# Three ways to split weights: adding transfers in place of VectorE subtractions in a decoder layer, and a new order on GpSimd

## The chip, the core and the metric

The kernel runs on one core of one Trainium2 chip. Its five engines work from queues of their own: TensorE (PE in the profile; PEld its weight loads), VectorE (DVE), ScalarE (ACT), GpSimd (POOL) and SyncE (SP, which here only issues transfers). The metric is the device time of one launch in microseconds (us). An engine runs its instructions strictly in the order of its queue: one that waits holds up all that stand behind it.

## The reference

One layer of a decoder trunk, in float32, on 256 prompt positions and 8 x 4 new sample positions. The 288 positions share all weights, so the kernel treats them as T = 288 columns.

```python
h = rmsnorm(x, norm1_g)
proj = h @ w_in + b_in                        # 2048 -> 3072
a, gate, z = proj[..., :1024], proj[..., 1024:2048], proj[..., 2048:]
u = a * sigmoid(gate)
c = silu(layernorm(depthwise_causal_conv(concat[hist_conv, u], conv_w, conv_b)))  # 31 taps
d = multiscale_pool(concat[hist_pool, z])     # means over 2, 4, 8, 16 positions, minus z
p = (d by group @ pool_w) * pool_scale        # 4 groups of 256 channels
x = x + concat[c, p] @ w_out                  # 2048 -> 2048
x = x + square(relu(rmsnorm(x, norm2_g) @ w_ff1)) @ w_ff2   # 2048 -> 8192 -> 2048
y = rmsnorm(x, norm_f)
```

The last 30 values of u and the last 15 of z go out too, as new state.

## The kernel before

**Products in three parts.** Channels lie on the 128 partitions, positions along the free axis. Each float32 operand is split into a high part, rounded to the fp32r type of TensorE, and a low part (the operand minus its high part), and each product is three matmuls of 128 x 128 by 128 x 288: high times high, low weight times high, high weight times low.

**Weights.** They come from HBM in halves of 512 KB (`wr`: 4 blocks of 128 rows x 256 columns). A half makes one weight tile: ScalarE casts it to the high part `whi` (L260), and the low part `wlo` is made in one of three ways (`split_part`, L252 on). V: one VectorE subtraction `raw - hi` (L265). G: two GpSimd subtractions of half a tile each (L268). D: ScalarE writes `-hi` into `wlo` (L262) and a transfer on GpSimd's queue adds the raw weights from HBM to it (L263). The table WAYS says which way each tile of a stage takes, in turn. There are 6 buffers for raw halves and 5 for weight tiles: the cast of tile n waits until TensorE's last matmul with tile n - 5 is done. TensorE uses a tile for 24 matmuls, a pool tile for 12. Tiles are numbered as they are made (`wlo14` is the low part of tile 14); L291 issues all matmuls.

**Order of the stages.** SEQUENCE gives the input projection and what hangs on it: "c0 c1 c2 c3 c4 p3 c5 p2 P3 c6 p1 P2 p0 P1 c7 P0". A c is one 128-channel pair of `a` and `gate` (4 tiles of halves, 2 in each of 2 loads, into one PSUM pair); behind it come the sigmoid, the 31 taps of the prompt on VectorE (`pc`, L448), and for the samples a product `prd` on GpSimd (L451) with a reduction on VectorE (L453). A p is the 256 channels of one pooling group: the scaled result `tz` (VectorE, L470), z (ScalarE, L473), the window sums `s` by doubling (GpSimd, L479; one doubling for group 0, four for group 3), division and subtraction for `d` (L483 to L487, GpSimd and VectorE), a cast to the high part of `dx` (ScalarE, L489) and its low part (VectorE, L490). A P multiplies `dx` of one group by its pool weights (`pp`, 12 matmuls). Then come the out-projection, first the half that reads pooled channels (stages w0 to w7, `ac<-dx`), then that of the convolution (`ac<-mx`), and the MLP.

**What sets the order.** A scheduler with a simulated timeline orders each engine's queue from the program's order; `later()` gives taps and products a low priority, and `tc.issue_after(x)` pins an instruction behind x. TensorE's order is pinned in places by `chain` and by `between`, which puts one product's matmuls into another's list.

Of the kernel before, what the change touches and what calls it, by code (L numbers as in the profile page):

```python
# [71 lines left out]

WAYS = {"c2": "GVGV", "c3": "GDGG", "c4": "GDGD", "p3": "GDDG", "c5": "GDGD", "c": "GGGV", "p": "GVVG", "w0": "VV", "w": "GG", "ff": "VV"}

# [12 lines left out]
def trunk_kernel(ctx: ExitStack, tc: tile.TileContext, io):  # L87
# [46 lines left out]
    def f32(t):  # L134
        return t.bitcast(F32)
# [27 lines left out]

    def load():

        src, raw = io["w"][next(blocks)], []
        for h in range(2):
            raw.append((raw_tile(), src[:, 4 * h : 4 * h + 4, :]))
            nc.sync.dma_start(*raw[-1])
        return raw  # L170
# [80 lines left out]

    turns = {}  # L252

    def split_part(raw, src, hi, lo, way):

        nc.scalar.copy(hi, raw)  # L260
        if way == "D":
            nc.scalar.activation(lo, f32(hi), AF.Copy, scale=-1.0)  # L262
            nc.gpsimd.dma_start(lo, src, accum_op=ALU.add)  # L263
        elif way == "V":
            nc.vector.tensor_tensor(lo, raw, f32(hi), op=ALU.subtract)  # L265
        else:
            for j in range(0, raw.shape[1], 2):
                nc.gpsimd.tensor_tensor(lo[:, j : j + 2, :], raw[:, j : j + 2, :], f32(hi[:, j : j + 2, :]), op=ALU.subtract)  # L268

# [25 lines left out]

    def gemm(banks, rhs, m_outer=False, between={}, classes="", by_part=False, gets=None, pairs=None):

# [12 lines left out]
        else:  # L310
# [3 lines left out]
            for k, m in pairs:  # L314
                begins[len(todo)] = (k, m) if m else k
                todo += [(k + d, m, w, x) for d, w, x in ((0, 0, 0), (1, 0, 0), (0, 1, 0), (1, 1, 0), (1, 0, 1), (0, 0, 1))]
        head = todo[: len(classes)]
        for j, c in enumerate(classes):
# [59 lines left out]
    def weight_groups():  # L378

        yield [lambda k, m, h=h: [t[:, m // 2, k % 2, m % 2 * P : (m % 2 + 1) * P] for t in firsts[4 * h + k // 2]] for h in range(2)]  # L380
        for kind, i in SEQUENCE[2:]:
            yield [pool_weights(i)] if kind == "P" else [split(load(), f"{kind}{i}") for _ in range(2)]
        for j in range(8):
            get = split(load(), f"w{j}")
            yield [lambda k, m, get=get: get(korder[k], m)]
        for _ in range(8):
            yield [split(load())]
        for _ in range(2 * DFF // 256):
            yield [split(load()) for _ in range(2)]
# [24 lines left out]

    cs, pcs = [], []
    sum_c = tmpp.tile([P, 2, T], F32, name="sum_c", tag="ag2", bufs=2)
# [10 lines left out]
    def conv_pair(i, banks):  # L427
# [9 lines left out]
        if i % 2 == 0:  # L437
            cs.append(actp.tile([P, 2, T], F32, name=nm("c"), tag="c", bufs=4))
        c = cs[i // 2][:, i % 2, :]
        with later():  # L440
# [9 lines left out]
            nc.scalar.activation(prd[:, :, :, CW], ones[:, 0 : NB * NS].rearrange("p (b t) -> p b t", t=NS), AF.Identity, bias=v("conv_b", i), scale=0.0)  # L450
            nc.gpsimd.tensor_tensor(prd[:, :, :, 0:CW], windows(us, CW), cwv[:, None, None, :].to_broadcast([P, NB, NS, CW]), op=ALU.mult)  # L451
            cso = c[:, SEQ:T]
# [11 lines left out]
    def pool_group(g):  # L464
# [18 lines left out]
        nc.gpsimd.tensor_tensor(first_sums, first_sums, rcnt[:, None, w - 2 : 2 * w - 3].to_broadcast([P, 2, w - 1]), op=ALU.mult)  # L483
        nc.vector.scalar_tensor_tensor(out=d[:, :, 0:SEQ], in0=s[:, :, PH:ZO], scalar=1.0 / w, in1=z[:, :, PH:ZO], op0=ALU.mult, op1=ALU.subtract)
        news = [x[:, :, ZO:ZL].rearrange("p m (b t) -> p m b t", t=ZS)[:, :, :, PH:] for x in (s, z)]
        nc.gpsimd.tensor_scalar(news[0], news[0], 1.0 / w, None, op0=ALU.mult)
        nc.gpsimd.tensor_tensor(d[:, :, SEQ:T].rearrange("p m (b t) -> p m b t", t=NS), news[0], news[1], op=ALU.subtract)  # L487
        dh, dl = act2("dx", tag="p", bufs=4)
# [36 lines left out]
    for kind, i in SEQUENCE[3:-1]:  # L525
        if (kind, i) == ("P", 1):
            continue
        if kind == "c":
            conv_pair(i, conv_products(i, classes=TURN if i == 5 else "", **(dict(gets=ahead(1), between={12: lambda: pool_products(1)}) if i == 7 else {})))
# [9 lines left out]
    gemm(each(bks[0]) + each(bks[1]), proj, gets=[lambda k, m: both_gets[m // 2][0](k, m % 2)], between={(0, 2): lambda: pool_products(0)}, classes="." * 36 + TURN, pairs=early + [(6, m) for m in range(4)])  # L539
    chain.clear()  # L540
# [241 lines left out]
```

## Time and profile before

| what | value |
|---|---|
| median of 3 runs | 1082.34 us (1081.94 to 1082.63) |
| the profiled execution | 1082.43 us, its span 1080.6 us |
| mean granted TensorE clock | 0.998 |
| PE busy | 1069.2 us, 8176 matmuls |
| DVE, ACT, POOL busy | 633.7, 479.0, 175.9 us |
| adding transfers (D) | 7, 512 KB each, median 7.8 us from issue to landing |

1.8 us of the profiled execution lie outside its span. In the page, the second part cuts the span into 40 slices of 27 us; a row of the timeline has start, duration, engine, line, operation, tiles and shapes, and in brackets the idle time before it with what ended it. A row "x4" stands for four instructions in a row, and its duration runs to the end of the last one.

### The profile page before, as it was taken

Reading aid. Unit: us, or ns where it says so; the run is one execution under the profiler, and the core shown is the slowest. Engines: PE = TensorE matmul, PEld = TensorE weight load, DVE = VectorE, ACT = ScalarE, POOL = GpSimd, SP = SyncE. Lnnn points to the kernel's source line nnn. Section 1 sums busy time; section 2 is a strip of 40 time slices with the busy share of each in tenths; the row PEclk is TensorE's granted clock in tenths of the full one; section 3 lists DMA queues with packets and bytes.
Section 4 is the critical chain, followed back from the end, with each engine's and each line's share of the span. In section 5 each row is a group of like instructions: output and inputs, shape, how many; then the busy total and the mean of one; then the engine's idle time right before and its main releaser. Section 6 shows DMA issues by size and latency. Waiting matters only on the chain.

```text
span 1080.6 us, 19528 instructions
## 1 busy us (share of the span) xinstructions
PE 1069.2 (99%) x8176; PEld 1067.9 (99%) x8176; DVE 633.7 (59%) x810; ACT 479.0 (44%) x588; POOL 175.9 (16%) x182
## 2 busy tenths in 40 slices
PE   9999999999999999999999999999999999999996
PEld 8999999999999999999999999999999999999996
DVE  7899999788654544444554444555544445554553
ACT  8654445665544433334443333444433334444441
POOL 0878979512000000000000000000000000000001
PEclk9999999999999999999999999999999999999999
DMA  9896478555555555555555555555555555555522
GB/s 326 288 263 182 145 187 247 177 171 173 162 173 166 169 175 163 170 173 165 170 174 164 170 170 167 171 173 162 173 168 167 173 171 164 173 166 170 172 79 88
DMA packets 58296, 190.71 MB, mean 176 GB/s; under 512 B 6240, under 2 KB 11232, under 8 KB 58208
## 3 DMA queue, kind: packets, MB, share of 16 engines
q1 hardware_dynamic: 56336, 184.35, 54.3%
q0 software_dynamic: 1008, 3.67, 1.9%
q8 instruction: 64, 1.05, 0.4%
q10 hardware_dynamic: 864, 1.44, 0.4%
q14 instruction: 24, 0.20, 0.0%
HBM read 185.16 MB, written 4.28 MB: 175 GB/s over the span
## 4 chain that ended last, share of the span: by engine, by line
PE 75%; issue 21%; ACT 2%; POOL 1%; DMA 1%; SPq 0%; POOLq 0%; DVE 0%
PE ac L291 74%; POOL wlo L268 1%; DMA wr<-in_w 1%; ACT whi L349 1%; PE pp L291 1%; DMA wlo<-in_w 1%; ACT hx L354 0%; ACT z_all L405 0%; POOL prd L451 0%; POOL xT L718 0%; ACT whi L260 0%; SPq L191 0%; POOLq L768 0%; DVE xT L691 0%; ACT whi L356 0%
## 5 line engine op out<-in xcount | busy, mean ns | idle before, releaser
L260 ACT CAST whi<-wr 128x1024 fp32r<-128x1024 f32 (+1 forms) x332 | 346.5, 1044 | 551.3 <-PE ac L291 536.7
L265 DVE TENSOR_TENSOR wlo<-wr,whi 128x1024 fp32r<-128x1024 f32 x288 | 353.5, 1227 | 348.1 <-ACT whi L260 348.1
L291 PE MATMUL ac<-ax,whi 128*128 128x288 f32 x2048 | 351.0, 292 | 0.0
L291 PE MATMUL ac<-fx,whi 128*128 128x288 f32 x2048 | 350.2, 292 | 0.0
L291 PEld LDWEIGHTS ac<-ax,whi 128*128 128x128 f32 x2048 | 296.0, 187 | 0.0
L291 PEld LDWEIGHTS ac<-fx,whi 128*128 128x128 f32 x2048 | 295.6, 187 | 0.0
L291 PE MATMUL ac<-ax,wlo 128*128 128x288 f32 x1024 | 217.3, 292 | 0.0
L291 PE MATMUL ac<-fx,wlo 128*128 128x288 f32 x1024 | 216.4, 292 | 0.0
L291 PEld LDWEIGHTS ac<-ax,wlo 128*128 128x128 f32 x1024 | 162.5, 187 | 0.0
L291 PEld LDWEIGHTS ac<-fx,wlo 128*128 128x128 f32 x1024 | 162.2, 187 | 0.0
L291 PE MATMUL ac<-hx,whi 128*128 128x288 f32 x768 | 131.9, 296 | 1.4 <-DVE hx L352 1.4
L718 POOL TENSOR_TENSOR xT<-xT,rf 128x288 f32<-128x288 f32 x4 | 3.1, 795 | 799.9 <-ACT rf L722 799.9
L291 PEld LDWEIGHTS ac<-hx,whi 128*128 128x128 f32 x768 | 112.6, 190 | 1.8 <-ACT hx L354 1.7
L268 POOL TENSOR_TENSOR wlo<-wr,whi 128x512 fp32r<-128x512 f32 x74 | 102.4, 1433 | 17.1 <-ACT whi L260 16.0
L448 DVE SCALAR_TENSOR_TENSOR pc<-u_all,vec,pc 128x256 f32<-128x256 f32 x232 | 99.3, 479 | 1.9 <-ACT pc L445 0.7
L291 PE MATMUL ac<-hx,wlo 128*128 128x288 f32 x384 | 80.4, 295 | 0.2 <-DMA wlo<-in_w 0.2
L291 PEld LDWEIGHTS ac<-hx,wlo 128*128 128x128 f32 x384 | 61.1, 189 | 0.4 <-DMA wlo<-in_w 0.4
L291 PE MATMUL ac<-dx,whi 128*128 128x288 f32 x256 | 46.8, 295 | 0.0
L291 PE MATMUL ac<-mx,whi 128*128 128x288 f32 x256 | 44.9, 293 | 0.0
L660 DVE SCALAR_TENSOR_TENSOR t<-ac,r 128x576 f32<-128x576 f32 x32 | 24.2, 757 | 25.4 <-PE ac L291 25.3
L291 PEld LDWEIGHTS ac<-dx,whi 128*128 128x128 f32 x256 | 38.4, 188 | 0.2
L291 PEld LDWEIGHTS ac<-mx,whi 128*128 128x128 f32 x256 | 37.5, 188 | 0.2 <-DVE xT L579 0.2
(129 smaller groups left out, 529.6 us busy)
## 6 DMA issues: line engine op xcount, KB each, us to landing
wr<-in_w SPq DMA_DIRECT2D x335, 512.0 KB, 3.8
wlo<-in_w POOLq DMA_DIRECT2D x7, 512.0 KB, 7.8
xT<-in_xT SPq DMA_DIRECT2D x8, 288.0 KB, 7.7
wr<-in_w SPq DMA_DIRECT2D x5, 256.0 KB, 3.9
out_u_out<-u_all SPq DMA_DIRECT2D x1, 1208.0 KB, 9.6
u_all<-in_hist_c SPq DMA_DIRECT2D x8, 136.0 KB, 5.3
out_z_out<-z_all SPq DMA_DIRECT2D x1, 668.0 KB, 9.2
z_all<-in_hist_p SPq DMA_DIRECT2D x4, 152.0 KB, 6.6
```

The costliest lines, as they stand in the source:

```text
L260: nc.scalar.copy(hi, raw)
L265: nc.vector.tensor_tensor(lo, raw, f32(hi), op=ALU.subtract)
L268: nc.gpsimd.tensor_tensor(lo[:, j : j + 2, :], raw[:, j : j + 2, :], f32(hi[:, j : j + 2, :]), op=ALU.subtract)
L291: last = nc.tensor.matmul(*args, **kw)
L349: nc.scalar.copy(hi[:, blocks[0]], raw[:, blocks[0]])
L448: nc.vector.scalar_tensor_tensor(out=dst, in0=up[:, w : w + SEQ], scalar=cwv[:, w : w + 1], in1=pc, op0=ALU.mult, op1=ALU.add)
L660: nc.vector.scalar_tensor_tensor(out=t, in0=bk[:, :, :T], scalar=0.0, in1=both(rows2[0]), op0=ALU.max, op1=ALU.mult)
L718: eng.tensor_tensor(xk, xk, r[:, None, :].to_broadcast([P, n, T]), op=ALU.mult)
```

## The change

- WAYS: the pooling groups p2, p1 and p0 take GDDG where they took GVVG (p3 had GDDG already): six VectorE subtractions go, six adding transfers come. c4 takes GGGD for GDGD. w0, the first stage of the out-projection, takes GV for VV. All in all 12 adding transfers in place of 7.
- The tap products `prd` are pinned behind the first adding transfers (list `added`). The taps of convolution pairs 2 and 3 are emitted one pair later (`waiting`).
- In a pooling group GpSimd's scaling and subtraction for the samples stand ahead of VectorE's `d`.
- The two halves of a pooled out-projection weight are loaded in the other order. GpSimd's subtractions made in c7 and after it are pinned behind the pooling of group 1, then 0 (`pooled`).
- P1 goes into c7 at k = 8 (12 before). In the first product of the out-projection P0 comes after 24 matmuls (36 before), and these 24 take all high weight parts first (`late`).
- The first product of the convolution half takes k = 0 and 2 for its first PSUM pair before the second pair begins (`mixed`): 24 matmuls, 12 before.

```diff
-WAYS = {"c2": "GVGV", "c3": "GDGG", "c4": "GDGD", "p3": "GDDG", "c5": "GDGD", "c": "GGGV", "p": "GVVG", "w0": "VV", "w": "GG", "ff": "VV"}
+WAYS = {"c2": "GVGV", "c3": "GDGG", "c4": "GGGD", "c5": "GDGD", "c": "GGGV", "p": "GDDG", "w0": "GV", "w": "GG", "ff": "VV"}
...
-    def load():
+    def load(order=(0, 1)):
...
-        for h in range(2):
+        for h in order:
...
-            nc.gpsimd.dma_start(lo, src, accum_op=ALU.add)
+            added.append(nc.gpsimd.dma_start(lo, src, accum_op=ALU.add))
...
-                nc.gpsimd.tensor_tensor(lo[:, j : j + 2, :], raw[:, j : j + 2, :], f32(hi[:, j : j + 2, :]), op=ALU.subtract)
+                with tc.issue_after(pooled[-1].ins) if pooled else nullcontext():
+                    nc.gpsimd.tensor_tensor(lo[:, j : j + 2, :], raw[:, j : j + 2, :], f32(hi[:, j : j + 2, :]), op=ALU.subtract)
...
+        todo[:late] = sorted(todo[:late], key=lambda p: p[2])
...
-            get = split(load(), f"w{j}")
-            yield [lambda k, m, get=get: get(korder[k], m)]
+            get = split(load((1, 0)), f"w{j}")
+            yield [lambda k, m, get=get: get(korder[k] ^ 4, m)]
...
+        while waiting:
+            taps(*waiting.pop())
+        if i in (2, 3):
+            waiting.append((i, up, us))
+        else:
+            taps(i, up, us)
...
-            nc.gpsimd.tensor_tensor(prd[:, :, :, 0:CW], windows(us, CW), cwv[:, None, None, :].to_broadcast([P, NB, NS, CW]), op=ALU.mult)
+            with tc.issue_after(added[max(0, min(2, i - 1))].ins):
+                nc.gpsimd.tensor_tensor(prd[:, :, :, 0:CW], windows(us, CW), cwv[:, None, None, :].to_broadcast([P, NB, NS, CW]), op=ALU.mult)
...
-        nc.vector.scalar_tensor_tensor(out=d[:, :, 0:SEQ], in0=s[:, :, PH:ZO], scalar=1.0 / w, in1=z[:, :, PH:ZO], op0=ALU.mult, op1=ALU.subtract)
...
-        nc.gpsimd.tensor_tensor(d[:, :, SEQ:T].rearrange("p m (b t) -> p m b t", t=NS), news[0], news[1], op=ALU.subtract)
+        last = nc.gpsimd.tensor_tensor(d[:, :, SEQ:T].rearrange("p m (b t) -> p m b t", t=NS), news[0], news[1], op=ALU.subtract)
+        newest[g] = last
+        nc.vector.scalar_tensor_tensor(out=d[:, :, 0:SEQ], in0=s[:, :, PH:ZO], scalar=1.0 / w, in1=z[:, :, PH:ZO], op0=ALU.mult, op1=ALU.subtract)
...
+        if i == 7:
+            pooled.append(newest[1])
...
-between={12: lambda: pool_products(1)}
+between={8: lambda: pool_products(1)}
...
+    pooled.append(newest[0])
...
-between={(0, 2): lambda: pool_products(0)}, classes="." * 36 + TURN, pairs=early + [(6, m) for m in range(4)])
+    mixed = [(k, m) for k in range(0, KT // 2, 2) for m in range(4)]
+    mixed.sort(key=lambda km: (km[0] // 4, km[1] // 2) if km[0] < 4 else (1, 0))
+late=24, between={4: lambda: pool_products(0)}, classes="." * 24 + TURN, pairs=early + [(6, m) for m in range(4)])
...
-    gemm(each(bks[0]) + each(bks[1]), mixc, gets=[lambda k, m: two_gets[m // 2][0](k, m % 2)])
+    gemm(each(bks[0]) + each(bks[1]), mixc, gets=[lambda k, m: two_gets[m // 2][0](k, m % 2)], pairs=mixed)
```

The new lines shift the line numbers of the changed kernel: its L269 is L268 above, L463 is L451, L491 is L479, L495 to L500 are L483 to L487, L502 and L503 are L489 and L490.

**GpSimd at the first adding transfer** (tile 14, of c3). Before:

```order
L268 TENSOR_TENSOR wlo13_604<-wr13_599,whi13_603 128x512 x2
L451 TENSOR_TENSOR prd1_667<-u_all_87,vec_85 128x32x31
L451 TENSOR_TENSOR prd2_708<-u_all_87,vec_85 128x32x31
L263 DMA wlo14_609<-in_w 128x1024
L268 TENSOR_TENSOR wlo15_618<-wr15_613,whi15_617 128x512 x2
```

Now:

```order
L269 TENSOR_TENSOR wlo13_604<-wr13_599,whi13_603 128x512 x2
L263 DMA wlo14_609<-in_w 128x1024
L463 TENSOR_TENSOR prd1_667<-u_all_87,vec_85 128x32x31
L463 TENSOR_TENSOR prd2_708<-u_all_87,vec_85 128x32x31
L269 TENSOR_TENSOR wlo15_618<-wr15_613,whi15_617 128x512 x2
```

The transfer has moved ahead of the first two tap products.

**ScalarE and VectorE around P3** (dx1 and d1 are those of group 3; tile 32 is p2's last, 34 to 37 are c6's; tz2 is p2's result). ScalarE before, then now:

```order
L260 CAST whi34_1556<-wr34_1552 128x1024
L260 CAST whi35_1561<-wr35_1554 128x1024
L445 ACTIVATE pc3_1057<-u_all_87,vec_85 128x256
L489 CAST dx1_1242<-d1_1237 128x576
L260 CAST whi36_1570<-wr36_1566 128x1024
L450 ACTIVATE prd8_2237<-ones_112,vec_85 128x32
L260 CAST whi37_1575<-wr37_1568 128x1024
```

```order
L260 CAST whi34_1558<-wr34_1554 128x1024
L260 CAST whi35_1563<-wr35_1556 128x1024
L260 CAST whi36_1572<-wr36_1568 128x1024
L461 ACTIVATE prd8_2244<-ones_112,vec_85 128x32
L260 CAST whi37_1577<-wr37_1570 128x1024
L502 CAST dx1_1242<-d1_1237 128x576
L485 ACTIVATE z_all_91<-tz2_1518,vec_85 128x256
```

VectorE before, then now:

```order
L490 TENSOR_TENSOR dx1_1242<-d1_1237,dx1_1242 128x2x288
L448 SCALAR_TENSOR_TENSOR pc3_1057<-u_all_87,vec_85,pc3_1057 128x256
L448 SCALAR_TENSOR_TENSOR pc2_719<-u_all_87,vec_85,pc2_719 128x256
L453 TENSOR_REDUCE c3_1056<-prd6_1406 128x32
```

```order
L482 TENSOR_TENSOR tz2_1518<-ac9_1415,rb1_250 128x576
L459 SCALAR_TENSOR_TENSOR pc2_851<-u_all_87,vec_85,pc2_851 128x256
L265 TENSOR_TENSOR wlo37_1578<-wr37_1570,whi37_1577 128x1024
L459 SCALAR_TENSOR_TENSOR pc3_1057<-u_all_87,vec_85,pc3_1057 128x256
L503 TENSOR_TENSOR dx1_1242<-d1_1237,dx1_1242 128x2x288
```

The high part of dx1 now stands behind the casts of tiles 36 and 37, its low part behind p2's tz2 and the low part of tile 37.

**GpSimd at p1's tiles** (38 to 41) and the pooling of group 2 (s5 to s7, d2). Before, then now:

```order
L479 TENSOR_TENSOR s5_1522<-z_all_91 128x422 x2
L479 TENSOR_TENSOR s6_1525<-s5_1522 128x420
L268 TENSOR_TENSOR wlo38_1686<-wr38_1681,whi38_1685 128x512 x2
L479 TENSOR_TENSOR s6_1525<-s5_1522 128x420
L456 TENSOR_TENSOR sum_c_251<-c1_634,c2_718 128x288
L479 TENSOR_TENSOR s7_1528<-s6_1525 128x416 x2
L268 TENSOR_TENSOR wlo41_1703<-wr41_1696,whi41_1702 128x512 x2
```

```order
L491 TENSOR_TENSOR s5_1524<-z_all_91 128x422 x2
L491 TENSOR_TENSOR s6_1527<-s5_1524 128x420 x2
L468 TENSOR_TENSOR sum_c_251<-c1_634,c2_718 128x288
L491 TENSOR_TENSOR s7_1530<-s6_1527 128x416 x2
L269 TENSOR_TENSOR wlo38_1688<-wr38_1683,whi38_1687 128x512 x2
L495 TENSOR_TENSOR s7_1530<-s7_1530,rcnt_131 128x2x7
L497 TENSOR_SCALAR s7_1530<-s7_1530 128x2x8x4
L263 DMA wlo39_1693<-in_w 128x1024
L498 TENSOR_TENSOR d2_1533<-s7_1530,z_all_91 128x2x32
L263 DMA wlo40_1702<-in_w 128x1024
```

Tiles 39 and 40 have become adding transfers here, behind all of group 2's sums.

More of the change, by code (lines that the diff above doesn't have):

```diff
@@ L250, in row_of_sums @@
         return row_of(psum, psum[:, 0, :T], *args), last
-    turns = {}
+    turns, added, newest, pooled = {}, [], {}, []
     def split_part(raw, src, hi, lo, way):
@@ L294, in mm, with gemm @@
         return last
-    def gemm(banks, rhs, m_outer=False, between={}, classes="", by_part=False, gets=None, pairs=None):
+    def gemm(banks, rhs, m_outer=False, between={}, classes="", by_part=False, gets=None, pairs=None, late=0):
         n = len(rhs)
@@ L412, in trunk_kernel @@
     rb = row("rb")
-    cs, pcs = [], []
+    cs, pcs, waiting = [], [], []
     sum_c = tmpp.tile([P, 2, T], F32, name="sum_c", tag="ag2", bufs=2)
@@ L438, in conv_pair, with taps @@
             cs.append(actp.tile([P, 2, T], F32, name=nm("c"), tag="c", bufs=4))
+        while waiting:
[4 more added lines that the diff above has]
+            taps(i, up, us)
+    def taps(i, up, us):
         c = cs[i // 2][:, i % 2, :]
@@ L527, in trunk_kernel @@
             continue
+        if i == 7:
+            pooled.append(newest[1])
         if kind == "c":
-            conv_pair(i, conv_products(i, classes=TURN if i == 5 else "", **(dict(gets=ahead(1), between={12: lambda: pool_products(1)}) if i == 7 else {})))
+            conv_pair(i, conv_products(i, classes=TURN if i == 5 else "", **(dict(gets=ahead(1), between={8: lambda: pool_products(1)}) if i == 7 else {})))
         elif kind == "p":
@@ L538, in trunk_kernel @@
     early.sort(key=lambda km: km[1] // 2)
-    gemm(each(bks[0]) + each(bks[1]), proj, gets=[lambda k, m: both_gets[m // 2][0](k, m % 2)], between={(0, 2): lambda: pool_products(0)}, classes="." * 36 + TURN, pairs=early + [(6, m) for m in range(4)])
+    mixed = [(k, m) for k in range(0, KT // 2, 2) for m in range(4)]
+    mixed.sort(key=lambda km: (km[0] // 4, km[1] // 2) if km[0] < 4 else (1, 0))
+    gemm(each(bks[0]) + each(bks[1]), proj, gets=[lambda k, m: both_gets[m // 2][0](k, m % 2)], late=24, between={4: lambda: pool_products(0)}, classes="." * 24 + TURN, pairs=early + [(6, m) for m in range(4)])
     chain.clear()
```

## The prediction

> **What bounds the kernel now.** I read the page first, then TensorE's waits, its timeline around them, and windows of equal length.
>
> ```profile
> PE 1069.2 (99%) x8176; PEld 1067.9 (99%) x8176; DVE 633.7 (59%) x810; ACT 479.0 (44%) x588; POOL 175.9 (16%) x182
> DVE  7899999788654544444554444555544445554553
> POOL 0878979512000000000000000000000000000001
> PE ac L291 <- DVE hx L352: 1.4, 1, 1.4
> PE warm L214 <- DVE cst L231: 1.0, 1, 1.0
> PE ac L291 <- DMA wlo<-in_w: 0.2, 1, 0.2
> PEld ac L291 <- DVE xT L579: 0.2, 1, 0.2
> ```
>
> TensorE is busy 1069.2 of 1080.6 us. Its waits total 2.6 us, and 2.4 of these lie in the start, which the change leaves alone. VectorE (slices of 27 us) is full only from about 54 to 190 us and GpSimd up to about 190 us, so 16% says nothing of that stretch. Whatever the change relieves, the time falls only by what TensorE loses now; whatever it makes late, the time rises by in full. What TensorE loses by less visible means stands in windows:
>
> ```profile
> 51.30:85.10 33.80, 33.80 (x256) 33.80 (x255) 31.17 (x75) 19.29 (x23) 26.08 (x22) 1.00 0.95 256
> 400.00:433.80 33.80, 33.80 (x262) 33.80 (x261) 15.73 (x14) 11.52 (x11) 0.00 (x0) 1.00 0.55 172
> 219.90:231.60 11.70, 11.70 (x90) 11.70 (x89) 7.09 (x8) 6.08 (x9) 0.00 (x0) 1.00 0.54 168
> 400.00:411.70 11.70, 11.70 (x92) 11.70 (x91) 5.65 (x5) 4.18 (x4) 0.00 (x0) 1.00 0.56 181
> ```
>
> Columns: us, busy time (with count) of PE, PEld, DVE, ACT and POOL, clock, DMA share, GB/s. A matmul at full pace takes 130 ns (two from 110.24 to 110.50, in the rows of term 2). Between 51.3 and 85.1 us there are 256 in the time that holds 262 later, though PE shows as busy: 6 x 0.13 = 0.8 us lost to a slower pace; from 219.9 us it is 2 x 0.13 = 0.26 us. Both slow stretches begin right after one of the two waits of 0.2 us.
>
> **Term 1, the first transfer (gain).** The first adding transfer of c3 waits on GpSimd behind two tap products:
>
> ```profile
> 40.16 4.33 POOL L451 TENSOR_TENSOR prd<-u_all,vec 128x992 f32<-128x992 f32 x2
> 44.41 5.97 DMA wlo<-in_w
> 49.55 0.68 PE L291 MATMUL ac<-hx,whi 128*128 128x288 f32 x4
> 50.42 0.54 PE L291 MATMUL ac<-hx,wlo 128*128 128x288 f32 x2 [0.20 <-DMA wlo<-in_w]
> ```
>
> Four matmuls from 49.55 end their turn at 50.07; the next begins at 50.42, so 0.35 us are lost, and its pair (0.54 for the usual 0.43) loses 0.1 more. In the new order the transfer stands ahead of both products: it is issued at about 40.2 and, with the same 5.97, lands at 46.2, 3.9 us early. At the slowest landing below (10.2) it is 50.4, and the stall stays. The two products come 0.9 us later (the issue's 0.87, term 3) and GpSimd's subtractions behind them start no later than now. If the slow pace goes with the stall, the gain is 0.45 + 0.8 + 0.1 (the same pace just after) = 1.35 us; if it comes from the full DMA (share 0.95), 0.5. I take **-1.35**, since the other slow stretch at 219.9 also follows a stall, at a DMA share of only 0.54.
>
> **Term 2, the pool product P3 (loss).** Six subtractions of p2, p1 and p0 leave VectorE. Here TensorE does not wait for VectorE, so the 6 x 1.36 us that they took hide under matmuls and bring nothing:
>
> ```profile
> L265 DVE TENSOR_TENSOR wlo<-wr,whi 128x1024 fp32r<-128x1024 f32 x10 | 13.6, 1364 | 0.4 <-ACT whi L260 0.4
> ```
>
> But the order around P3 (12 matmuls on group 3's pooled input dx) changes. Before, ScalarE's cast to dx's high part stands ahead of two weight casts and ends 4 us early; VectorE's low part of dx follows at once.
>
> ```profile
> 104.50 1.06 ACT L260 CAST whi<-wr 128x1024 fp32r<-128x1024 f32 x1 [1.98 <-PE ac L291]
> 105.96 0.66 ACT L489 CAST dx<-d 128x576 fp32r<-128x576 f32 x1
> 110.81 1.03 ACT L260 CAST whi<-wr 128x1024 fp32r<-128x1024 f32 x1
> 106.85 1.79 DVE L490 TENSOR_TENSOR dx<-d,dx 128x576 fp32r<-128x576 f32 x1
> 110.24 0.42 PE L291 MATMUL ac<-hx,whi 128*128 128x288 f32 x2
> 110.50 0.42 PE L291 MATMUL pp<-dx,whi 128*128 128x288 f32 x2
> 111.02 0.68 PE L291 MATMUL pp<-dx,whi 128*128 128x288 f32 x4
> ```
>
> In the new order the cast of weight tile 37 stands ahead of the cast of dx. Tile 37 goes into the buffer of tile 32, the last of p2, so its cast waits for p2's last matmul, and P3, the next on TensorE, waits for the cast of dx behind it. Worked out: p2's last matmul starts at 110.24 + 0.13 = 110.37. The lag from such a matmul to the cast is 0.37: tile 30's last one starts 49 turns before 110.50 (two tiles of 24 lie between), at 104.13, and the cast it frees starts at 104.50. So cast 37 runs 110.74 to 111.77, the cast of dx ends at about 112.4, and P3 starts 1.95 us late. Its fifth and sixth matmuls need dx's low part. On VectorE that now stands behind the subtraction of tile 37, which waits for cast 37, and a tap:
>
> ```profile
> L490 DVE TENSOR_TENSOR dx<-d,dx 128x576 fp32r<-128x576 f32 x4 | 4.3, 1068 | 0.0
> L448 DVE SCALAR_TENSOR_TENSOR pc<-u_all,vec,pc 128x256 f32<-128x256 f32 x123 | 52.4, 477 | 0.4
> ```
>
> Subtraction 111.85 + 1.36 = 113.2, tap 113.7, dx's low part 114.75, against 111.02 now: **+3.8** in total, the 1.95 within it. The bounds: the shortest row of the low part known from the trace of before (0.75, as in the row of L590 below) gives 3.3, the longest (1.79) 4.5. Nothing else may hide it: all of c6 is queued behind P3 on TensorE.
>
> **Term 3, added transfers that land late (loss).** Six adding transfers come, one goes (c4); their issue waits in GpSimd's order. Landing times now:
>
> ```profile
> DMA to landing us min/median/max: 6.0/7.8/10.2
> 68.90 0.87 POOL L263 DMA_DIRECT2D wlo<-in_w  x1 [2.04 <-ACT wlo L262]
> 79.32 0.43 PE L291 MATMUL ac<-hx,wlo 128*128 128x288 f32 x2
> 104.52 0.42 PE L291 MATMUL ac<-hx,wlo 128*128 128x288 f32 x2
> 127.92 0.42 PE L291 MATMUL ac<-hx,wlo 128*128 128x288 f32 x2
> 131.04 0.42 PE L291 MATMUL ac<-hx,wlo 128*128 128x288 f32 x2
> 113.50 2.71 POOL L479 TENSOR_TENSOR s<-z_all 128x422 f32<-128x422 f32 x2
> 124.85 2.98 POOL L268 TENSOR_TENSOR wlo<-wr,whi 128x512 fp32r<-128x512 f32 x2
> L479 POOL TENSOR_TENSOR s<-s 128x420 f32<-128x420 f32 x6 | 6.7, 1134 | 0.0
> L456 POOL TENSOR_TENSOR sum_c<-c,c 128x288 f32<-128x288 f32 x1 | 0.8, 802 | 0.0
> ```
>
> One landing of 10.2 (68.90 to 79.1) was the second of two close issues and came 0.2 us before its use at 79.32, so there is no room already. p1's first transfer (tile 39) now stands behind group 2's sums, a sum of convolutions, tile 38's subtraction and two small operations: from 113.3, 2.71 + 2.27 + 0.80 + 2.27 (the last doubling at the same 1134 ns a piece) + 2.98 + 0.5 = 11.5, so issue at 124.8 and landing at 130.8 (6.0) to 132.6 (7.8), for a use at 127.92. That alone would cost 2.9 to 4.7 us; but the use has moved by the 3.8 of term 2 to 131.7, which leaves 0 to 0.9. The next (tile 40) is issued some 1.3 later, at 126.1, and lands at 133.9 to 136.3 for a use at 131.04 + 3.8 = 134.8: 0 to 1.5, not added to tile 39's stall but overlapping it. Tile 31 in p2 (issue about 95.1, as the second of two) lands at 102.9 to 105.3 for 104.52: 0 to 0.8. Together 0 to 2.5; I take **+1.0**.
>
> The Trainium skill, page "DMA: Bandwidth & Descriptors", section "Anatomy of one DMA — SWDGE (gpsimd) path", fits such a transfer as 2.0 us plus its bytes over 436 GB/s, an estimate of 3.2 us for 512 KB. By that term 3 would be zero and the sum 1.0 us lower; the trace's 6.0 to 10.2 contradict it, since these also read the destination, and I go by the trace.
>
> **Term 4, the slow pace behind new stalls (loss).** After the stall at 50.42 it cost 0.8 us, after the wait at 219.9 it cost 0.26. Three new stalls: 0 to 1.4, I take **+0.6**.
>
> **Term 5, the convolution half of the out-projection (gain).** Its first product needs the second PSUM buffer, which VectorE frees late:
>
> ```profile
> 218.09 0.75 DVE L590 TENSOR_TENSOR mx<-n,mx 128x576 fp32r<-128x576 f32 x1
> 218.75 0.74 DVE L579 TENSOR_TENSOR xT<-xT,ac 128x576 f32<-128x576 f32 x1
> 219.19 0.90 PE L291 MATMUL ac<-mx,whi 128*128 128x288 f32 x4
> ```
>
> 24 matmuls on the first buffer, in place of 12, put the need for the second at 221.0, past L579's end at 219.5; the inputs that come in earlier (mx of k = 2, 3) are ready at 218.84 for 219.5. Gain 0.2 + 0.25 = **-0.45** (0 to 0.6).
>
> **At nothing:** w0's one subtraction on GpSimd, P1 and P0 put earlier, c4's GGGD, the moved taps. Each has 2 to 5 us of matmuls as cover by the same rows; should one of GpSimd's subtractions of c7 be late, it costs its 2.98.
>
> **Sum** against the profiled execution (1082.43 us, span 1080.6): 1082.43 - 1.35 + 3.8 + 1.0 + 0.6 - 0.45 = 1086.0. It lies 0.09 above the median of the runs, 1082.34, so **1085.9 us**. About 0.2%, or 2.2 us, is what a measurement tells from no change: faster is below 1080.2, slower above 1084.5.
>
> **Rivals.** (a) **P3 does not stall**: the cast of dx gets by because GpSimd and ScalarE run ahead of what I reckon. For it: nothing but that the tile's buffer might be free sooner. Against: both casts are on one engine, in order, and the buffer is held by the very matmuls before P3. Price: the gains alone, 1082.34 - 1.8 = 1080.5; but tile 39's 2.9 us then show unless its landing is hidden too. It is faster than before only if both are. (b) **Near balance**: P3 costs its least, 3.3, nothing else is late, and the gains reach 2.0: 1082.34 + 3.3 - 2.0 = 1083.6. For it: a stall lets every later transfer catch up. Against: tile 31 comes before P3. (c) **Transfers stack**: each pair of adding transfers (tiles 30/31, 39/40, 44/45) lands as the one of 10.2; tile 31 costs 0.8, 40 1.5, 45 0.6 and the slow pace 1.4: 1082.34 - 1.8 + 3.8 + 2.9 + 1.4 = 1088.6. (d) **The clock drops** in the pauses:
>
> ```profile
> 1072.00:1075.00 3.00, 0.00 (x0) 0.00 (x0) 3.00 (x5) 0.33 (x1) 2.59 (x4) 1.00 0.76 280
> 1076.00:1079.00 3.00, 0.00 (x0) 0.00 (x0) 0.00 (x0) 0.00 (x0) 0.00 (x0) 0.50 0.96 368
> ```
>
> After 3 us with no matmul the clock is still 1.00, between 3 and 4 us later 0.50. P3's stall is in two pieces of about 1.9 us with four matmuls between, so I expect no drop. If it came, and lasted as long as it took to come, 3 to 4 us at half pace cost 1.5 to 2.0 more: 1087.7. The Trainium skill, page "TensorE: Matmul & The Clock Gate", section "Part 1: The HAM clock gate (the "warmup" mystery)", says that one idle window of about 3.4 us halves the rate; the two windows agree with it, and by it too the pieces are too short.
>
> **How the numbers follow.** The forecast, with P3 at 3.3 to 4.5 and some late transfers, has 0.66 and covers 1084.5 to 1087.6. (a) has 0.07, of which 0.05 faster and 0.02 within; (b) 0.15 within; (c) 0.08; (d) 0.04. Faster 0.05, same 0.17, slower 0.78. The range 1083.2 to 1088.6 holds the forecast's, most of (b) and (c) to its price.
>
> **What would show it.** Step 2 is right if PE's waits list P3's product (pp) with a wait for ACT dx of about 2 us and one for DVE dx of 1.4 to 2.6 near 110 us, and wrong if pp has none. Step 1 is right if the wait for the transfer near 50 us is gone and 51 to 85 us holds 260 matmuls or more; 256 again would lay the pace to the DMA. Step 3 shows as waits of PE for wlo<-in_w at about 103, 131 and 135 us. Step 5 is right if the wait for xT L579 is gone. The forecast fails if the dx cast precedes cast 37 in time, or if tile 39's transfer lands much later than 132.

## The result and the profile after

The changed kernel takes 1092.36 us (median of 4 runs, 1091.52 to 1093.26) against 1082.49 us: a ratio of 1.0092, 95% interval 1.0075 to 1.0109. It is slower, as forecast, but by 9.9 us and not by 3.6; the time lies outside the range of 1083.2 to 1088.6. The profiled execution took 1093.26 us with a span of 1091.5 us.

From the page of the changed kernel, the row of busy times and the granted clock in 40 slices:

```profile
PE 1073.3 (98%) x8176; PEld 1071.4 (98%) x8176; DVE 632.9 (58%) x803; ACT 484.0 (44%) x593; POOL 181.3 (17%) x191
PEclk9999899999999999999999999999999999999998
```

From its view of TensorE's waits (us in total, times, longest us), all but the two of the start:

```profile
PE pp L292 <- DVE dx L503: 2.9, 1, 2.9
PE pp L292 <- ACT dx L502: 2.8, 1, 2.8
PE ac L292 <- DMA wlo<-in_w: 0.9, 2, 0.6
```

P3 (`pp`) waits twice, for the two instructions that the prediction named; together 5.7 us. The third row is the adding transfers of p3 (tiles 22 and 23). One slice of the clock, from 109 to 136 us, has fallen below nine tenths. The timeline of TensorE shows the waits, and what came with them:

```profile
75.83 0.54 PE L292 MATMUL ac<-hx,wlo 128*128 128x288 f32 x2 [0.58 <-DMA wlo<-in_w]
79.61 0.53 PE L292 MATMUL ac<-hx,wlo 128*128 128x288 f32 x2 [0.31 <-DMA wlo<-in_w]
...
110.63 0.42 PE L292 MATMUL ac<-hx,whi 128*128 128x288 f32 x2
113.90 0.85 PE L292 MATMUL pp<-dx,whi 128*128 128x288 f32 x2 [2.84 <-ACT dx L502]
118.10 1.33 PE L292 MATMUL pp<-dx,whi 128*128 128x288 f32 x4 [2.87 <-DVE dx L503]
120.19 0.68 PE L292 MATMUL ac<-hx,whi 128*128 128x288 f32 x2
```

Two matmuls in a row took 0.42 us at 110.63 and take 0.68 at 120.19. The windows of the changed kernel (columns as in the prediction) say why:

```profile
112.00:114.00 2.00, 0.10 (x1) 0.10 (x1) 2.00 (x4) 1.16 (x2) 2.00 (x3) 0.75 0.21 59
118.10:123.40 5.30, 5.30 (x22) 5.30 (x23) 4.87 (x12) 1.84 (x3) 5.30 (x7) 0.51 0.30 89
```

and the same stretch of the kernel before:

```profile
118.10:123.40 5.30, 5.30 (x43) 5.30 (x43) 5.19 (x10) 2.10 (x2) 5.30 (x5) 1.00 0.41 132
```

The clock was halved at about 113 us, in P3's first pause, and came back at 123.3 us: 22 matmuls in the time of 43. "PE busy" is 5.30 of 5.30 in both rows; only the count and the clock tell them apart.

For the whole program I took from each trace what the matmuls' starts lose against 130 ns a matmul, in stretches that hold the same matmuls by number (named by the times they have in the kernel before; us):

| kernel | 49-100 | 110-125 (P3) | 125-157 | 157-196 | 196-300 |
|---|---|---|---|---|---|
| before | 1.41 | 0.00 | 0.00 | 0.09 | 1.37 |
| changed | 1.75 | 9.42 | 0.83 | 0.42 | 0.89 |

The difference is 10.4 us of the 10.9 by which the spans differ. P3 alone is 9.4.

### The profile page after: what moved, and what is told of

The parts are those of the page before. It is cut to its first block, busy times and chain, and to the rows that moved or that the text cites. A ratio compares the mean times of both kernels' runs of the same rounds, so it can differ in the third digit from the quotient of the medians.

```text
span 1091.5 us, 19546 instructions
## 1 busy us (share of the span) xinstructions
PE 1073.3 (98%) x8176; PEld 1071.4 (98%) x8176; DVE 632.9 (58%) x803; ACT 484.0 (44%) x593; POOL 181.3 (17%) x191
## 3 DMA queue, kind: packets, MB, share of 16 engines
q10 hardware_dynamic: 864, 1.44, 0.4%
## 4 chain that ended last, share of the span: by engine, by line
PE 76%; issue 20%; DVE 2%; DMA 1%; POOL 0%; POOLq 0%; ACT 0%; DVEq 0%
PE ac L292 75%; DMA wlo<-in_w 1%; DVE pc L459 1%; PE pp L292 1%; DVE wlo L265 0%; DMA wr<-in_w 0%; POOL xT L736 0%; DVE d L500 0%; DVE c L465 0%; DVE dx L503 0%; PE norm L292 0%; POOLq L786 0%; DVE xT L709 0%; DVE tz L482 0%; ACT whi L351 0%
## 5 line engine op out<-in xcount | busy, mean ns | idle before, releaser
L265 DVE TENSOR_TENSOR wlo<-wr,whi 128x1024 fp32r<-128x1024 f32 (+1 forms) x281 | 348.1, 1239 | 347.3 <-ACT whi L260 347.3
L269 POOL TENSOR_TENSOR wlo<-wr,whi 128x512 fp32r<-128x512 f32 x78 | 104.2, 1403 | 19.8 <-ACT whi L260 18.3
```

## The experiments

All kernels compute the whole reference. Times stand against the kernel before in the same job (its median lay between 1081.49 and 1082.11 us), ratios with their 95% interval.

### Only the six ways undone

```diff
-"p": "GDDG"
+"p3": "GDDG", "p": "GVVG"
```

> The changed kernel with one part undone: p2, p1 and p0 take GVVG again (no adding transfers there); everything else stays changed. Theory A (the six new adding transfers of p2, p1 and p0 crowd GpSimd's queue, so that group 3's sums and d, and with them P3, come late): P3's two pauses near 111 and 115 us (2.8 and 2.9 us) vanish, the clock stays at 1.00, and the time falls from 1092.4 to about 1082.5 (1081.7 to 1083.5); the two waits for a transfer near 75 and 79 us stay, since those belong to p3. Theory B (the moved taps and the new order of GpSimd's and VectorE's work in a pooling group make P3 late, whatever way the weights take): the pauses stay and the time stays above 1089.

1085.58 us, ratio 1.0034 (1.0021 to 1.0047): 3.7 us slower than the kernel before in place of 9.9, so 6.1 us go with the six ways. P3's pauses are gone and dx1's cast stands ahead of tile 35's, so theory A holds for P3. But the forecast of 1082.5 missed: a new pause stands at P0, which waits for VectorE:

```profile
PE pp L292 <- DVE dx L515: 1.8, 1, 1.8
```

The first window holds that pause; the other two are 3.41 us each, the clock's own steps (last section):

```profile
167.30:169.20 1.90, 0.24 (x2) 0.01 (x1) 1.90 (x4) 0.93 (x1) 1.90 (x2) 1.00 0.97 362
166.92:170.33 3.41, 1.65 (x13) 1.42 (x12) 3.41 (x7) 1.83 (x2) 3.41 (x3) 1.00 0.95 360
170.33:173.74 3.41, 3.41 (x17) 3.41 (x16) 3.38 (x10) 0.77 (x2) 3.41 (x4) 0.50 0.97 369
```

One pause of 1.9 us, from one matmul's turn to the next, halved the clock for 3.4 us (170.33 to 173.74), and that after the matmuls had begun again. The stretch 157-196 loses 5.1 us in all.

### Only the six ways done, on the kernel before

```diff
-"p": "GVVG"
+"p": "GDDG"
```

> The kernel before with one part of the change alone: p2, p1 and p0 take GDDG; no tap is moved, no pin is added. In the order that follows, the cast of dx1 stands behind p2's z on ScalarE and d1 behind the first sums of group 2 on GpSimd, later still than in the changed kernel. Theory A: P3 pauses for longer than in the changed kernel, the clock drops, and the time is 1092 to 1098; the early wait at 50 us stays. Theory B: no pause, 1082 to 1084.

1094.08 us, ratio 1.0114 (1.0099 to 1.0129), theory A again. One wait now, since the cast is later still, and the half clock behind it:

```profile
PE pp L291 <- ACT dx L489: 7.6, 1, 7.6
```

The six ways alone are enough; the pins and moved taps are not the cause. At most they soften it (P3's stretch loses 10.6 us here and 9.4 in the changed kernel; the intervals of the two ratios overlap).

### Matmuls in P3's pauses

The cut is shortened.

```diff
+        for _ in range(21):    # ahead of P3, pinned behind p2's last matmul
+            nc.tensor.matmul(bk[:, 1, :T], hx[0][0][:, :P], hx[0][0], start=True, stop=True)
         gemm(each(bk), halves(dd[g]))   # and 22 more between its fourth and fifth matmul
```

> The changed kernel with 21 matmuls ahead of P3's first and 22 between its fourth and fifth, which read an input that has long been there and write a PSUM bank that P3 overwrites: TensorE works in the pauses and nothing else is changed. Theory C (the clock dropped to 0.50 because TensorE paused; the half pace from 114 to 123 us and the slower pace of 133 ns up to about 180 us are both paid for the pause): clock 1.00 throughout, time down by 2.9 us for the half pace, to about 1089.5, and by 1.2 more, to 1088.3, if the slower pace follows the pause too. If the clock does not matter, 1092.4 stays.

1089.85 us, ratio 1.0077 (1.0062 to 1.0092): 8.0 us slower than the kernel before in place of 9.9, though 43 matmuls more run. The clock holds:

```profile
112.00:122.00 10.00, 9.35 (x69) 8.89 (x68) 9.86 (x18) 4.43 (x9) 10.00 (x10) 1.00 0.44 132
```

In the stretch 110-125 it loses 1.61 us and spends 43 x 0.13 = 5.59 on the added matmuls, 7.20 against 9.42: the half clock cost 2.2 us, the lateness of dx1 with the slower pace behind it the other 7.2. The slower pace (133 ns) up to about 180 us stayed at 0.82 us: it needs no long pause, the remaining 0.3 and 0.7 us were enough. That half of theory C falls.

### One tap product moved

```diff
-            with tc.issue_after(added[max(0, min(2, i - 1))].ins):
+            with tc.issue_after((newest[3] if i == 5 else added[max(0, min(2, i - 1))]).ins):
```

> The changed kernel with one GpSimd product moved: the tap product of convolution pair 5 is pinned behind group 3's last pooling subtraction; the 12 adding transfers stay. In the queues that follow, the cast of dx1 now stands ahead of the cast of tile 37 and VectorE's low part of dx1 ahead of p2's tz. Theory A1 (P3 is late by the order of a few instructions around it, not by the adding transfers as such): both pauses of P3 go or fall below 1 us in all, no clock drop, time 1082 to 1086, the rest over 1082 being late transfers of p1 (tile 39 and 40). Theory A2 (GpSimd is simply too full with the transfers, so d1 comes late in any order): the first pause stays at 2 us or more and the time stays above 1088.

1087.11 us, ratio 1.0049 (1.0032 to 1.0066). Two pauses of 0.7 and 1.3 us remain at P3, no drop of the clock, and p1's and p0's transfers show:

```profile
PE ac L292 <- DMA wlo<-in_w: 1.9, 4, 0.7
...
PE pp L292 <- DVE dx L503: 1.3, 1, 1.3
...
PE pp L292 <- ACT dx L502: 0.7, 1, 0.7
```

It lies between the theories: most of P3's loss is a matter of order (9.42 becomes 2.89 in that stretch), not all, and behind it the transfers, with the slower pace, cost 2.62 in the next stretch, where the changed kernel lost 0.83.

### One VectorE subtraction moved

In the changed kernel the chain to P3 starts 11 us earlier than the prediction looked. From its timelines of VectorE, GpSimd and ScalarE:

```profile
99.77 2.72 DVE L265 TENSOR_TENSOR wlo<-wr,whi 128x512 fp32r<-128x512 f32 x1
99.58 2.35 POOL L491 TENSOR_TENSOR s<-s 128x408 f32<-128x408 f32 x2
102.90 0.50 ACT L436 ACTIVATE tg<-ac,vec 128x288 f32<-128x288 f32 x1 [2.83 <-DVE ac L434]
103.30 1.04 ACT L260 CAST whi<-wr 128x1024 fp32r<-128x1024 f32 x1
104.42 2.54 POOL L269 TENSOR_TENSOR wlo<-wr,whi 128x512 fp32r<-128x512 f32 x2 [2.49 <-ACT whi L260]
...
111.46 1.03 ACT L260 CAST whi<-wr 128x1024 fp32r<-128x1024 f32 x1
112.36 0.78 POOL L498 TENSOR_TENSOR d<-s,z_all 128x64 f32<-128x64 f32 x1
113.17 0.67 ACT L502 CAST dx<-d 128x576 fp32r<-128x576 f32 x1 [0.69 <-POOL d L498]
114.71 1.97 DVE L265 TENSOR_TENSOR wlo<-wr,whi 128x1024 fp32r<-128x1024 f32 x1
117.00 1.05 DVE L503 TENSOR_TENSOR dx<-d,dx 128x576 fp32r<-128x576 f32 x1
```

The half-size subtraction of tile 33 took 2.72 us; the very same one took 0.94 in the kernel before. It started beside GpSimd's work and ended 0.6 us after the second of GpSimd's two doublings. Behind it waited the second gate product (L434), the sigmoid, cast 34, and with them GpSimd for 2.49 us, which then was late with group 3's `d`: the cast of dx1 waited 0.69 us longer for `d` than for cast 37. The Trainium skill, page "SBUF — State Buffer", section "Who interferes with whom", says that a VectorE instruction with two SBUF inputs contends with a GpSimd instruction that reads SBUF, and that the contention is an exclusive lock. The trace agrees: the subtraction waited out both doublings, and it took 2.73 to 2.74 us in three other kernels where it met them too. The edit pins it behind pair 5's writes of u (the cut is shortened: the condition that picks tile 33 is left out):

```diff
+            with tc.issue_after(newest["u"].ins):   # tile 33 only
                 nc.vector.tensor_tensor(lo, raw, f32(hi), op=ALU.subtract)
```

> The changed kernel with one VectorE instruction later: the subtraction for P3's pool weights (tile 33, 128x512) is pinned behind convolution pair 5's writes of u. In the changed kernel it starts at 99.8 us beside GpSimd's last doubling of group 3 (99.6 to 101.9), takes 2.7 us where it took 0.94 before, and holds up the second gate product, the sigmoid, the cast of tile 34 and GpSimd behind it. The cast of dx1 still stands behind the cast of tile 37 in the queue. Theory D (the mis-sized part of P3's pauses comes from this blocked subtraction; what is left then is the 3.8 us that the order of the casts gives): the subtraction takes 0.8 to 1.0 us, P3's two pauses come to about 2.2 and 1.2 us, the clock stays at 1.00 or nearly, and the time is about 1087 (1086 to 1088.5). If the blocked subtraction delays nothing that matters, the pauses stay near 2.8 and 2.9 us and the time near 1092.

1089.34 us, ratio 1.0074 (1.0059 to 1.0089). From its timelines of VectorE and ScalarE:

```profile
99.92 0.68 DVE L266 TENSOR_TENSOR wlo<-wr,whi 128x512 fp32r<-128x512 f32 x1
109.19 1.04 ACT L260 CAST whi<-wr 128x1024 fp32r<-128x1024 f32 x1 [2.07 <-PE ac L293]
110.14 0.67 ACT L503 CAST dx<-d 128x576 fp32r<-128x576 f32 x1
110.68 2.04 DVE L266 TENSOR_TENSOR wlo<-wr,whi 128x1024 fp32r<-128x1024 f32 x1
112.65 1.44 DVE L504 TENSOR_TENSOR dx<-d,dx 128x576 fp32r<-128x576 f32 x1
```

and from its view of TensorE's waits:

```profile
PE pp L293 <- DVE dx L504: 2.5, 1, 2.5
PE pp L293 <- ACT dx L503: 1.8, 1, 1.8
```

The time lies above theory D's range. The subtraction now starts as the doublings end and takes 0.68 us, the cast of dx follows cast 37 at once, and P3's first matmul comes 1.91 us late: the 1.95 of the prediction. The second pause stayed long (2.5, not 1.2), mostly because the next subtraction took 2.04 us where 1.36 was reckoned, and the low part of dx 1.44 for 1.07. So theory D explains 2.4 us of P3's stretch (9.42 becomes 7.05). 2.0 of them are P3's lateness; the rest is that the clock, which still fell, came back after 6.8 us and not after 10.2.

### Both single moves

```diff
+            with tc.issue_after(newest["u"].ins):   # tile 33 only
                 nc.vector.tensor_tensor(lo, raw, f32(hi), op=ALU.subtract)
...
-            with tc.issue_after(added[max(0, min(2, i - 1))].ins):
+            with tc.issue_after((newest[3] if i == 5 else added[max(0, min(2, i - 1))]).ins):
```

> The changed kernel with both single moves: the subtraction of tile 33 behind the writes of u, and pair 5's tap product behind group 3's last pooling subtraction. All 12 adding transfers stay. P3's pauses go (below 0.5 us in all). What is left against the kernel before is then the price of the transfers themselves: if GpSimd's queue is ahead by the time that P3 no longer pauses, waits of p1's tiles 39 and 40 stay at 0.7 and 0.9 us and the time is 1084 to 1085; if P3's pauses had only hidden the transfers' lateness, these waits grow by what P3 gives back and the time stays at 1086 to 1087.

1085.09 us, ratio 1.0032 (1.0020 to 1.0044). One pause of 0.8 us remains at P3, where less than 0.5 was forecast, and the transfers' two waits stay, 0.9 us the longer:

```profile
PE ac L293 <- DMA wlo<-in_w: 1.4, 2, 0.9
...
PE pp L293 <- DVE dx L504: 0.8, 1, 0.8
```

With P3 nearly mended the kernel is still slower than before, by 3.6 us in the median. In its profile P3's stretch loses 1.4 us and the one of p1 and p0 2.8; in the stretch 49-100 it loses only 0.09 us: here term 1's gain is whole.

### Only the first transfer moved, on the kernel before

```diff
-            nc.gpsimd.tensor_tensor(prd[:, :, :, 0:CW], ...)
+            with tc.issue_after(added[0].ins) if added and i < 2 else nullcontext():
+                nc.gpsimd.tensor_tensor(prd[:, :, :, 0:CW], ...)
```

> The kernel before with one part of the change alone: the first two tap products on GpSimd are pinned behind the first adding transfer (tile 14); all ways stay as before. Predicted as term 1: the wait at 50 us and the slower pace up to 85 us go, 1.35 us. Theory E (later transfers of p3, tiles 22 and 23, have so little room that they take the gain back): waits for wlo appear near 75 and 79 us, 0.3 to 0.7 us each, with a slower pace behind them, and the time is 1081.2 to 1082.2 against 1081.84 before; if the gain stays whole, 1080.5.

1086.07 us, ratio 1.0044 (1.0032 to 1.0057): 4.6 us slower, outside both forecasts. The wait at 50 us is gone, and others have come, one for c4's first transfer (tile 18, at 62 us) and a row of them for VectorE from 160 us on:

```profile
PE ac L291 <- DVE dx L503: 0.8, 1, 0.8
PE ac L291 <- DMA wlo<-in_w: 0.8, 1, 0.8
PE pp L291 <- DVE dx L491: 0.5, 1, 0.5
```

So term 1's gain is gone at 62 us, and the stretch 157-196 loses 3.6 us where the kernel before loses 0.1. Why VectorE is late there, the next run helps to see.

### Three edits together, on the kernel before

```diff
-"p3": "GDDG"
+"p3": "GDGD"
...
+            with tc.issue_after(added[0].ins) if added and i < 2 else nullcontext():
...
-    gemm(each(bks[0]) + each(bks[1]), mixc, gets=[...])
+    gemm(each(bks[0]) + each(bks[1]), mixc, gets=[...], pairs=mixed)
```

> The kernel before with three edits: the two tap products behind the first adding transfer, the mixed order in the first product of the convolution half (24 matmuls on the first PSUM pair ahead of the second), and p3's ways GDGD for GDDG, so that its two transfers (tiles 22 and 24) are issued further apart. If all of it holds: no wait at 50, 75 or 79 us and none for xT near 219 us; 1081.84 - 1.4 - 0.45 = 1080.0 (1079.5 to 1080.8). If the transfers are slow for another reason than being close together, a wait near 75 us stays and the time is 1080.8 to 1081.8.

1085.78 us, ratio 1.0038 (1.0026 to 1.0051). This lies outside both forecasts. No wait near 75 us, but one of 1.8 us at 62 us (tile 18) and the same row of waits for VectorE: 3.62 us in the stretch 157-196. It does not tell whether the distance of two transfers matters, since the wait came earlier.

An earlier TensorE is not what makes VectorE late there: the matmul that starts at 157.04 us in the kernel before starts at 157.29 here, and the loss is that of the run before. But VectorE's own instructions are longer. The low part of group 2's dx, in the kernel before and then here:

```profile
131.44 0.99 DVE L490 TENSOR_TENSOR dx<-d,dx 128x576 fp32r<-128x576 f32 x1
130.92 2.58 DVE L491 TENSOR_TENSOR dx<-d,dx 128x576 fp32r<-128x576 f32 x1
```

Here it started 0.2 us after a tap product on GpSimd that ran to 132.9 us; before, it met only the end of one. Group 0's took 1.50 us for 0.74. That this alone makes the 3.6 us was not tested.

The pause of 1.8 us at 62 us left the clock whole, though the equally long one of the first experiment halved it. The same steps of 3.41 us, which the pause straddles here:

```profile
59.63:63.04 3.41, 2.03 (x16) 1.80 (x14) 3.41 (x10) 2.02 (x3) 3.41 (x3) 1.00 0.99 305
63.04:66.46 3.42, 3.00 (x22) 3.00 (x23) 3.42 (x8) 0.58 (x1) 1.96 (x2) 1.00 1.04 266
```

### Only the mixed order, on the kernel before

```diff
-    gemm(each(bks[0]) + each(bks[1]), mixc, gets=[...])
+    gemm(each(bks[0]) + each(bks[1]), mixc, gets=[...], pairs=mixed)
```

> The kernel before with one part of the change alone, the one farthest from the rest: the mixed order in the first product of the convolution half (24 matmuls on the first PSUM pair ahead of the second). The queues up to 200 us stay as they were. Term 5 as predicted: the wait for xT near 219 us goes, with the slower pace behind it, 0.45 us (0.2 at the least), so 1081.0 to 1081.3 against 1081.5. If it is hidden or moves the wait elsewhere: no change. A difference this small shows in the windows from 200 to 300 us rather than in the median.

1081.63 against 1082.11 us, ratio 0.9995 (0.9987 to 1.0004): no difference that the runs can tell. In the trace the wait for xT is gone, and the stretch 196-300 loses 0.89 us for 1.37. The 0.48 us are term 5.

### Half of the swap, and two variations

On the changed kernel, p2, p1 and p0 take one transfer each, and VectorE keeps three subtractions:

```diff
-"p": "GDDG"
+"p3": "GDDG", "p": "GVDG"
```

> The changed kernel with half of the swap: p2, p1 and p0 take GVDG for GDDG, so three adding transfers instead of six, never two in a row, and three of the six VectorE subtractions stay away. In the queues that follow, the cast of dx1 stands ahead of the casts of tiles 35 to 37. Theory F (VectorE has no slack near 160 us as soon as TensorE comes earlier, which took the gain away in the kernels with all six subtractions; GpSimd and the transfers have none near 110 to 145 us, which took it away in those with none; half of each has room on both): no pause of P3, no wait for wlo near 130 and 145 us, no pause near 160 to 170 us, and a time of 1079.8 to 1081.3, the first below the kernel before. If one transfer for each group is already late, or three subtractions already too many, a wait of 0.5 to 2 us stands at one of these places and the time is 1082 to 1084.

1085.10 us, ratio 1.0026 (1.0017 to 1.0036), above both forecasts, as the next two runs are above theirs. No pause at P3 and none at 160 us, but one transfer of p1 is late, and the pause halves the clock again (4.36 us in the stretch 125-157). Its issue in GpSimd's timeline and its use in TensorE's:

```profile
125.11 0.86 POOL L263 DMA_DIRECT2D wlo<-in_w  x1
...
132.35 0.53 PE L292 MATMUL ac<-hx,wlo 128*128 128x288 f32 x2 [1.94 <-DMA wlo<-in_w]
```

Then with p1 back at two subtractions:

```diff
-"p": "GVDG"
+"p2": "GVDG", "p1": "GVVG", "p0": "GVDG"
```

> As e12_half, with p1 back to GVVG: the one transfer that was late there (tile 40, issued at 125.1 us, used at 130.1, landed at 132.3) is a VectorE subtraction again; p2 and p0 keep GVDG, so two adding transfers instead of six and four subtractions instead of none. Theory F: no wait for wlo after 100 us, no pause, clock 1.00, and 1085.1 less the 2.1 us of that wait, some 2 us of half pace and 1 us of slower pace behind it: 1079.8 to 1080.8, below the kernel before (1082.1 in the last runs). If VectorE has no room for a fourth subtraction, a pause of 0.5 us or more for dx or pp stands between 125 and 175 us and the time is 1081 to 1084.

1084.65 us, ratio 1.0028 (1.0018 to 1.0039). The late transfer is gone and VectorE is late in its place, with the writes of u that free a PSUM buffer:

```profile
PE ac L292 <- DVE u_all L438: 1.5, 1, 1.5
```

Then with GpSimd in that transfer's place, and pair 6's tap product behind group 2's `d`:

```diff
-"p1": "GVVG"
+"p1": "GVGG"
...
-            with tc.issue_after(added[max(0, min(2, i - 1))].ins):
+            with tc.issue_after((newest[2] if i == 6 else added[max(0, min(2, i - 1))]).ins):
```

> As e12_half, with the late transfer of p1 (tile 40) replaced by two GpSimd subtractions (p1: GVGG; p2 and p0 keep GVDG) and the tap product of pair 6 pinned behind group 2's last pooling subtraction. VectorE has three subtractions as in e12_half, where it had no pause near 170 us; GpSimd gets 2.5 us more near 122 us and had 2.7 and 0.9 us idle after 134 us there. Theory F: no wait for wlo after 100 us, no pause of P2 or P3, clock 1.00, 1079.8 to 1081.3, with the two waits near 75 and 79 us (0 to 1.2 us in all, which come and go between runs) as the rest. If GpSimd has no room either, a pause for dx of P2 near 137 us, or a later one, of 0.5 us or more stands there and the time is 1081.5 to 1084.

1089.56 us, ratio 1.0073 (1.0059 to 1.0087). Up to 143 us this is the best of all: only the 0.09 us of the stretch 49-100. Then the transfer of tile 45, which stands on GpSimd behind the work that was put there, comes 5.4 us late (GpSimd's timeline, then TensorE's waits). Part of this is its landing, 10.6 us after issue; with the 7.0 of the run with half of the swap it would be about 1.8:

```profile
138.66 0.89 POOL L263 DMA_DIRECT2D wlo<-in_w  x1
```

```profile
PE ac L292 <- DMA wlo<-in_w: 5.4, 1, 5.4
```

So in these orders each of the three ways meets a limit between 100 and 175 us: VectorE with four or six subtractions, GpSimd's queue with two more halves, the transfers with three or six. The kernel before, with six subtractions in its own order, loses 0.1 us there. No kernel beat it by more than the runs can tell.

## Why the prediction was right or wrong

**Direction and place: right.** P3 is where the time went; TensorE waits there for ScalarE's dx and then for VectorE's dx, as step 2 said it would show.

**Term 2, P3, +3.8: mis-sized; it measured 9.4.** The wait and its place were right, its size was not. P3's fifth matmul, the first that needs dx's low part, came 6.7 us late (118.10 for 111.41), and 2.7 more were lost behind it. Three amounts were missing. First, 2.0 us: the chain was followed back only to cast 37. That part was right (1.91 us against 1.95 with one subtraction moved), but the cast of dx had a second input, GpSimd's `d`, and it was later, from one subtraction that GpSimd blocked; without that the fifth matmul came 4.7 us late. Secondly, 0.9 us: VectorE's durations were taken as means over a stretch where GpSimd does other work at the same moment; beside it, the subtraction of tile 37 took 1.97 us for 1.36. Thirdly, the 2.7 behind: the clock, 2.2 us by the run with matmuls in the pauses, and the slower pace. The term's lower bound, 3.3, was a slip (3.8 less the 0.32 between 1.07 and 0.75 is 3.5); nothing hangs on it.

**Rival (d), the clock, 0.04: it happened,** on top of the forecast and near the price given there (2.2 us for 1.5 to 2.0). The step that failed is the condition. From "clock 1.00 after 3 us without a matmul" I concluded that pauses of 1.9 us are too short. That row shows only that the drop comes late. A pause of 1.9 us halved the clock one microsecond after it had ended (ways undone). Length alone does not settle it: one just as long (three edits), one of 1.7 us (p1 back at GVVG) and two of 0.9 and 1.4 us in a row (one product moved) did not.

**Term 1, -1.35: the mechanism held, the gain did not.** In the two kernels where no later transfer of that stretch was late it was 1.32 us (1.41 becomes 0.09). In the changed kernel's profile two later transfers took it back: with TensorE 1.3 us earlier, tiles 22 and 23 came 0.6 and 0.3 us late, and the stretch loses 1.75. The row was in the prediction, landing at 79.1 for a use at 79.32; that its 0.2 us of slack had to be set against term 1's own gain was left out. These landings vary from run to run (8.7 to 11.2 us after issue in the nine profiles of the changed kernel and its variants), so the waits there came to between nothing and 1.2 us.

**"VectorE's relief brings nothing": right for the kernel before, which loses 0.1 us between 157 and 196 us.** The four kernels that leave it four or six subtractions in another order lose 2.9 to 5.1 us there, those with three or none 0.1 to 0.45. The runs with three edits and with the first transfer moved show longer VectorE instructions ahead of it; what of the loss they cause stays open.

**Term 3, +1.0 (0 to 2.5): not seen in the changed kernel, since P3's pauses hid it,** as its lower bound said. With P3 mended it is 2.8 us with the slower pace behind it.

**Term 4, +0.6 (0 to 1.4): 0.8 us from 125 to 157 us and 0.3 behind that.** Right within its bounds. What was put at nothing (w0, P1 and P0, c4, the moved taps) shows no wait in the changed kernel.

**Term 5, -0.45: 0.48,** in the changed kernel and alone.

## What to carry to other kernels

When an edit makes one engine earlier, set its gain against the slack of every later wait, also of engines that the profile shows as never waited for; an engine that is full and just in time looks the same as one that does not matter. Follow a late instruction back through all its inputs, and price a VectorE instruction that will run beside GpSimd's work by rows where it did so, not by a mean. A stall of about 2 us on TensorE may bring a half clock behind it, which "PE busy" does not show: count the matmuls.

## What the runs showed of the hardware

- **The clock can drop after a pause of 1.9 us, and need not.** The Trainium skill, page "TensorE: Matmul & The Clock Gate", section "Part 1: The HAM clock gate (the "warmup" mystery)", gives one idle window of about 3.4 us as the condition. Here about half of that sufficed; the measurement decides. In each trace the granted clock changes only at times that lie whole multiples of 3.41 us apart: it was half for 3.41 us in the run with the ways undone, for 6.83 with one subtraction moved and for 10.24 in the changed kernel (113.01 to 123.25). From 20 us to the last large product, the full clock was halved after every such step in which TensorE was busy for 1.66 of the 3.41 us or less (1.65 with the ways undone, 1.47 with half of the swap, 1.46 in the changed kernel), and after none with 1.93 or more (1.93 with p1 back at GVVG, 2.03 with one product moved and with three edits). So it matters how a pause lies to the steps. The steps lie at other times in every trace, so the same pause may cost a half clock in one run and not in the next. This is read from the traces; no run was made to test it.
- **A VectorE subtraction beside GpSimd's work can take four times as long:** that of tile 33 took 0.68 us where it started as GpSimd's doublings ended, 0.94 in the kernel before beside GpSimd's subtractions, 2.72 where it met two doublings.
- **A slower pace of 133 ns a matmul follows most waits,** those of 0.3 us as well as those of 3 us, for tens of us, at a clock of 1.00. It did not follow the longest but one, of 5.4 us (GpSimd in the transfer's place). What sets and ends it stays open; no run here tested it.
- **Adding transfers of 512 KB took 5.8 to 11.2 us** from issue to landing. The second of two close ones was often the longest (11.2), but one that stood alone took 10.6.
